# One decoder step on one core: place of the last pooling products, paired first groups of the output projection, earlier LayerNorm steps, another product for the mean, and new places for the operand order

## The chip, the cores and the metric

The kernel runs on one NeuronCore of a Trainium2 chip. The metric is the device time of one launch in microseconds (us), lower is better. Times are the median of several runs. A span is the time from the first to the last instruction of one profiled execution.

## What is computed

One layer of a hybrid decoder for a prompt of 256 positions and 8 sequences with 4 new positions each; both go through the same weights, so the kernel treats them as T = 288 columns. Cut to what matters:

```python
h = rmsnorm(x, norm1_g)
proj = h @ w_in + b_in                       # 2048 -> 1024 (a), 1024 (gate), 1024 (z)
u = a * sigmoid(gate)
c = silu(layernorm(depthwise_conv31(u) + conv_b) * ln_g + ln_b)   # mean, variance over 1024
d = multiscale_pool(z)                       # windows 2, 4, 8, 16; four groups of 256 channels
p = blockdiag(d, pool_w) * pool_scale        # four 256x256 products
x = x + concat(c, p) @ w_out
h2 = rmsnorm(x, norm2_g)
x = x + square(relu(h2 @ w_ff1)) @ w_ff2     # 2048 -> 8192 -> 2048
y = rmsnorm(x, norm_f)
```

Outputs are y and the new histories of u and z. All arrays are float32.

## The kernel before, in words

Channels lie on the 128 partitions, the 288 columns along the free axis. Every weight block (1024 rows by two times 128 columns) is loaded by SyncE's queue in two halves `wr` of 128x1024 (a ring of 6), and each half is split into `whi`, rounded to fp32r, and `wlo`, the rest (rings of 5). ScalarE (ACT) casts `whi` (L274), and VectorE (DVE, L279), GpSimd (POOL, L282) or a DMA (L277) forms `wlo`, by the table `WAYS`. The activations are split in the same way into a high and a low part. `gemm` (L310) then makes each result of three products: high by high, low weight by high, high weight by low. All products of the model go through `mm` (L302), so L305 is the line of nearly every matmul.

A tile of split activations has four rows of 288 numbers: the high parts of two neighbouring k are rows 1 and 2, the low parts rows 3 and 0. So (k + x) % 2, with x = 0 for the high and 1 for the low part, tells whether a product reads an odd or an even row. I call this the class of a product. The usual order in `gemm` alternates the classes 0, 1, 0, 1. A `gemm` called with `classes` takes the first products of its list in another order, so that their classes follow that string; `TURN` (L70), 48 digits long, is the one that is used. Before, five calls have it: the first two of the program, c5, and output group 2 of either half of `w_out`; the second group of `w_ff1` has it too, behind 12 products in the usual order.

The order of the groups of the input projection is `SEQUENCE` (L45): c0 to c7 are the conv columns (96 products each: 16 k, 2 halves, 3 kinds), p3 to p0 the pooling columns, and P3 to P0 the small products with `pool_w` (12 each). It ends in `p0 P1 c7 P0`. Then come 8 groups `g` of 256 output columns over the pooling half of `w_out` (48 products each), 8 over the conv half, and the two matrices of the MLP in four chunks.

While `chain` holds an instruction, every matmul is tied behind the one before it. At P1 (L540) it is cleared, and from there the scheduler of the tile framework places the matmuls by its own idea of time; it is filled again nowhere. `between` (L339) calls a function at the start of a given k. It puts the three LayerNorm steps on TensorE (PE) in the midst of groups 5, 6 and 7: `ln_mean` (L556, two float32 products with a matrix of ones), `ln_sums` (L561, which subtracts the mean, squares and sums on DVE and ACT and makes three products `pt` of one column), and `ln_rows` (L575, three products `pt` that spread the result to all partitions). DVE, ACT, POOL and SyncE each work in the order that the scheduler wrote. DVE's conv taps (`pc`, L461, 30 for each of 8 channel blocks) fill its gaps until the mean.

The conv result of c7 goes into `u_all` (L449), which reads the last PSUM (accumulator memory) tile `ac` of the input projection. The two tiles `ac` of the pool `acc` are used in turn, so an output group can't begin before the reader of the group two before it is done. The result of `pool_products(g)` is split by ACT (L514) and DVE (L515) into `dx`, the operand of the output projection.

Of the kernel before, what the change touches and what calls it, by code (L numbers as in the profile page):

```python
# [86 lines left out]
def trunk_kernel(ctx: ExitStack, tc: tile.TileContext, io):  # L87
# [222 lines left out]
    def gemm(banks, rhs, m_outer=False, between={}, classes="", by_part=False):  # L310
# [3 lines left out]
        gets = ready.pop(0)  # L314
# [9 lines left out]
        else:  # L324
            pairs = [(k, m) for k in range(0, n, 2) for m in range(len(banks))]
# [213 lines left out]
    for kind, i in SEQUENCE[3:]:  # L539
        if (kind, i) == ("P", 1):  # L540
            chain.clear()
        if kind == "c":
            conv_pair(i, conv_products(i, classes=TURN if i == 5 else ""))
        elif kind == "p":
            pool_group(i)
        else:
            pool_products(i)
    load_table(AF.Sqrt, f32(mixp[1][0])[:, 0:1])
# [6 lines left out]

    def ln_mean():  # L556
        norm["mean"] = ms("pmean")[:, 0, :T]
        mm(norm["mean"], ones, sum_c[:, 0, :], start=True, stop=False)
        return mm(norm["mean"], ones, cs[-1][:, 1, :], start=False, stop=True)

    def ln_sums():  # L561
        ssc = None
        for c in cs:
            nc.vector.tensor_tensor(c, c, norm["mean"][:, None, :].to_broadcast([P, 2, T]), op=ALU.subtract)
# [14 lines left out]
    BETWEEN = {5: {4: ln_mean}, 6: {6: ln_sums}, 7: {2: ln_rows}}  # L579
    behind = nullcontext()  # L580
    for g in range(8):
        bk = bank2()
        with behind:
            last = gemm(each(bk), [mixp[k] for k in korder], between=BETWEEN.get(g, {}), classes=TURN if g == 2 else "")
# [19 lines left out]
    last = None  # L604
    for g in range(8):
        bk = bank2()
        last = gemm(each(bk), mixc, classes=TURN if g == 2 else "")
# [30 lines left out]
    def second_rows():  # L638

        hl = actp.tile([P, 4, T], F32R, name="hl", tag="act")  # L640
        hi, lo = hl[:, 1, :], hl[:, 0, :]
        nc.scalar.copy(hi, ss2)
        nc.vector.tensor_tensor(lo, ss2, f32(hi), op=ALU.subtract)
        bk, r2 = ms("mean2"), row("r2")
        mean, root = bk[:, 0, :T], bk[:, 1, :T]
        mm(mean, means, hi, start=True, stop=False)
        last = mm(mean, means, lo, start=False, stop=True)
# [136 lines left out]
```

## Time and profile before

| what | value |
|---|---|
| median of 3 runs (lowest, highest) | 1084.95 us (1084.12, 1085.59) |
| span of the profiled execution | 1082.8 us |
| the execution's own time | not given by the page; the median of the runs is 2.15 us over the span |
| PE busy, matmuls | 1071.5 us (99%), 8198 |
| DVE, ACT, POOL busy | 635.4, 479.0, 173.6 us |
| mean granted TensorE clock | 0.997 |

A matmul's busy time (292 to 296 ns) overlaps that of its neighbours. The time that one adds is the distance between two starts. The chain of waits lists runs of matmuls with start, length and count, so length divided by count is that distance. A busy share of 99% therefore says little; small losses show as a longer distance or as a hole between two rows.

### The profile page before, as it was taken

Reading aid. Unit: us, or ns where it says so; the run is one execution under the profiler, and the core shown is the slowest. Engines: PE = TensorE matmul, PEld = TensorE weight load, DVE = VectorE, ACT = ScalarE, POOL = GpSimd, SP = SyncE. Lnnn points to the kernel's source line nnn. Section 1 sums busy time; section 2 is a strip of 40 time slices with the busy share of each in tenths; the row PEclk is TensorE's granted clock in tenths of the full one; section 3 lists DMA queues with packets and bytes.
Section 4 is the critical chain, followed back from the end, with each engine's and each line's share of the span. In section 5 each row is a group of like instructions: output and inputs, shape, how many; then the busy total and the mean of one; then the engine's idle time right before and its main releaser. Section 6 shows DMA issues by size and latency. Waiting matters only on the chain.

```text
span 1082.8 us, 19572 instructions
## 1 busy us (share of the span) xinstructions
PE 1071.5 (99%) x8198; PEld 1069.9 (99%) x8198; DVE 635.4 (59%) x818; ACT 479.0 (44%) x585; POOL 173.6 (16%) x180
## 2 busy tenths in 40 slices
PE   9999999999999999999999999999999999999996
PEld 9999999999999999999999999999999999999996
DVE  8899999678655544445544444545544445554553
ACT  8654445475544433334443333444433334444441
POOL 0878979512000000000000000000000000000001
PEclk9999999999999999999999999999999999999998
DMA  9896468545555555555555555555555555555522
GB/s 325 281 273 185 137 196 239 176 152 177 173 164 170 172 166 169 174 164 169 171 168 168 175 165 169 174 167 167 174 165 168 174 169 165 173 166 168 173 78 88
DMA packets 58296, 190.71 MB, mean 176 GB/s; under 512 B 6240, under 2 KB 11232, under 8 KB 58208
## 3 DMA queue, kind: packets, MB, share of 16 engines
q1 hardware_dynamic: 56336, 184.35, 53.9%
q0 software_dynamic: 1008, 3.67, 1.9%
q8 instruction: 64, 1.05, 0.4%
q10 hardware_dynamic: 864, 1.44, 0.4%
q14 instruction: 24, 0.20, 0.1%
HBM read 185.16 MB, written 4.28 MB: 175 GB/s over the span
## 4 chain that ended last, share of the span: by engine, by line
PE 77%; issue 20%; ACT 1%; DVE 0%; DMA 0%; POOL 0%; POOLq 0%
PE ac L305 77%; PE pp L305 1%; DMA wr<-in_w 0%; ACT whi L274 0%; POOL xT L720 0%; ACT n L595 0%; DVE wlo L279 0%; PE pt L305 0%; PE pmean L305 0%; POOLq L770 0%; DVE xT L695 0%; DVE n L592 0%; ACT whi L364 0%; ACT mx L597 0%; DVE hx L367 0%
## 5 line engine op out<-in xcount | busy, mean ns | idle before, releaser
L274 ACT CAST whi<-wr 128x1024 fp32r<-128x1024 f32 (+1 forms) x332 | 348.0, 1049 | 551.4 <-PE ac L305 533.5
L279 DVE TENSOR_TENSOR wlo<-wr,whi 128x1024 fp32r<-128x1024 f32 x288 | 353.1, 1226 | 348.5 <-ACT whi L274 348.5
L305 PE MATMUL ac<-ax,whi 128*128 128x288 f32 x2048 | 351.0, 292 | 0.0
L305 PE MATMUL ac<-fx,whi 128*128 128x288 f32 x2048 | 350.2, 292 | 0.0
L305 PEld LDWEIGHTS ac<-ax,whi 128*128 128x128 f32 x2048 | 296.0, 187 | 0.0
L305 PEld LDWEIGHTS ac<-fx,whi 128*128 128x128 f32 x2048 | 295.6, 187 | 0.0
L305 PE MATMUL ac<-ax,wlo 128*128 128x288 f32 x1024 | 217.4, 292 | 0.0
L305 PE MATMUL ac<-fx,wlo 128*128 128x288 f32 x1024 | 216.4, 292 | 0.0
L305 PEld LDWEIGHTS ac<-ax,wlo 128*128 128x128 f32 x1024 | 162.6, 187 | 0.0
L305 PEld LDWEIGHTS ac<-fx,wlo 128*128 128x128 f32 x1024 | 162.3, 187 | 0.0
L305 PE MATMUL ac<-hx,whi 128*128 128x288 f32 x768 | 131.8, 295 | 1.2 <-DVE hx L367 1.2
L720 POOL TENSOR_TENSOR xT<-xT,rf 128x288 f32<-128x288 f32 x4 | 3.1, 795 | 800.1 <-ACT rf L724 800.1
L305 PEld LDWEIGHTS ac<-hx,whi 128*128 128x128 f32 x768 | 112.1, 190 | 1.4 <-ACT hx L369 1.4
L282 POOL TENSOR_TENSOR wlo<-wr,whi 128x512 fp32r<-128x512 f32 x74 | 100.3, 1410 | 35.3 <-ACT whi L274 34.3
L461 DVE SCALAR_TENSOR_TENSOR pc<-u_all,vec,pc 128x256 f32<-128x256 f32 x232 | 99.5, 483 | 1.9 <-ACT pc L458 0.7
L305 PE MATMUL ac<-hx,wlo 128*128 128x288 f32 x384 | 80.1, 294 | 0.0
L305 PEld LDWEIGHTS ac<-hx,wlo 128*128 128x128 f32 x384 | 61.1, 190 | 0.0
L305 PE MATMUL ac<-dx,whi 128*128 128x288 f32 x256 | 46.0, 296 | 0.0
L305 PE MATMUL ac<-mx,whi 128*128 128x288 f32 x256 | 45.1, 294 | 0.1
L664 DVE SCALAR_TENSOR_TENSOR t<-ac,r 128x576 f32<-128x576 f32 x32 | 24.2, 758 | 25.1 <-PE ac L305 25.1
L305 PEld LDWEIGHTS ac<-dx,whi 128*128 128x128 f32 x256 | 38.0, 188 | 0.2
L305 PEld LDWEIGHTS ac<-mx,whi 128*128 128x128 f32 x256 | 37.5, 188 | 0.6 <-ACT mx L597 0.4
(133 smaller groups left out, 533.6 us busy)
## 6 DMA issues: line engine op xcount, KB each, us to landing
wr<-in_w SPq DMA_DIRECT2D x335, 512.0 KB, 3.8
wlo<-in_w POOLq DMA_DIRECT2D x7, 512.0 KB, 7.7
xT<-in_xT SPq DMA_DIRECT2D x8, 288.0 KB, 7.3
wr<-in_w SPq DMA_DIRECT2D x5, 256.0 KB, 3.6
out_u_out<-u_all SPq DMA_DIRECT2D x1, 1208.0 KB, 9.3
u_all<-in_hist_c SPq DMA_DIRECT2D x8, 136.0 KB, 6.2
out_z_out<-z_all SPq DMA_DIRECT2D x1, 668.0 KB, 9.9
z_all<-in_hist_p SPq DMA_DIRECT2D x4, 152.0 KB, 7.5
```

The lines of the kernel that those rows point to most:

```text
L274: nc.scalar.copy(hi, raw)
L279: nc.vector.tensor_tensor(lo, raw, f32(hi), op=ALU.subtract)
L282: nc.gpsimd.tensor_tensor(lo[:, j : j + 2, :], raw[:, j : j + 2, :], f32(hi[:, j : j + 2, :]), op=ALU.subtract)
L305: last = nc.tensor.matmul(*args, **kw)
L461: nc.vector.scalar_tensor_tensor(out=dst, in0=up[:, w : w + SEQ], scalar=cwv[:, w : w + 1], in1=pc, op0=ALU.mult, op1=ALU.add)
L664: nc.vector.scalar_tensor_tensor(out=t, in0=bk[:, :, :T], scalar=0.0, in1=both(rows2[0]), op0=ALU.max, op1=ALU.mult)
L720: eng.tensor_tensor(xk, xk, r[:, None, :].to_broadcast([P, n, T]), op=ALU.mult)
```

## The change

- `SEQUENCE` is walked without P1 and P0. P1 is called inside c7, before k = 12. P0 is called inside the first output groups. `chain` is now cleared only behind these.
- Output groups 0 and 1 of the pooling half are one `gemm` over four accumulators: 36 products of group 0 (all that don't need P0), P0, then the 36 of group 1, and the 24 that use P0's result; the last 60 have `TURN` on their first 48.
- Groups 0 and 1 of the conv half are likewise one `gemm`, with k outermost and `TURN` on the first 48 products; they are tied behind group 7's last product.
- `ln_mean` moves from k = 4 to k = 0 of group 5, `ln_sums` from k = 6 to k = 4 of group 6, `ln_rows` from k = 2 to k = 0 of group 7. Groups 5 and 7 get `TURN`, group 2 of the pooling half loses it.
- The mean: DVE adds the last two parts, ACT rounds the sum, DVE forms the rest, and two fp32r products with `means` (ones divided by 2048) replace the two float32 products; the subtraction becomes a scalar_tensor_tensor with factor -2.
- The weights' list `ready` may run one group further ahead (`ahead`). In `second_rows` the root lies in SBUF rather than PSUM.

```diff
-        gets = ready.pop(0)
+        gets = gets or ready.pop(0)
...
-                if m == 0:
-                    begins[len(todo)] = k
+                begins[len(todo)] = (k, m) if m else k
...
-            todo[j] = next(p for p in head if (p[0] + p[3]) % 2 == int(c))
+            todo[j] = next(p for p in head if c == "." or (p[0] + p[3]) % 2 == int(c))
...
-    for kind, i in SEQUENCE[3:]:
+    for kind, i in SEQUENCE[3:-1]:
         if (kind, i) == ("P", 1):
-            chain.clear()
+            continue
         if kind == "c":
-            conv_pair(i, conv_products(i, classes=TURN if i == 5 else ""))
+            conv_pair(i, conv_products(i, classes=TURN if i == 5 else "", **(dict(gets=ahead(1), between={12: lambda: pool_products(1)}) if i == 7 else {})))
...
+    early = [(k, m) for k in (0, 2, 4) for m in range(4)]
+    early.sort(key=lambda km: km[1] // 2)
+    gemm(each(bks[0]) + each(bks[1]), proj, gets=[lambda k, m: both_gets[m // 2][0](k, m % 2)], between={(0, 2): lambda: pool_products(0)}, classes="." * 36 + TURN, pairs=early + [(6, m) for m in range(4)])
+    chain.clear()
...
+    def mean_rows(total, name):
+        hl = actp.tile([P, 4, T], F32R, name=nm("hl"), tag="act")
+        hi, lo = hl[:, 1, :], hl[:, 0, :]
+        nc.scalar.copy(hi, total)
+        nc.vector.tensor_tensor(lo, total, f32(hi), op=ALU.subtract)
+        mean = ms(name)[:, 0, :T]
+        mm(mean, means, hi, start=True, stop=False)
+        return mean, mm(mean, means, lo, start=False, stop=True)
...
-        mm(norm["mean"], ones, sum_c[:, 0, :], start=True, stop=False)
-        return mm(norm["mean"], ones, cs[-1][:, 1, :], start=False, stop=True)
+        nc.vector.tensor_tensor(total, total, cs[-1][:, 1, :], op=ALU.add)
+        norm["half"], last = mean_rows(total, "pmean")
...
-    BETWEEN = {5: {4: ln_mean}, 6: {6: ln_sums}, 7: {2: ln_rows}}
+    BETWEEN = {5: {0: ln_mean}, 6: {4: ln_sums}, 7: {0: ln_rows}}
...
-            last = gemm(each(bk), [mixp[k] for k in korder], between=BETWEEN.get(g, {}), classes=TURN if g == 2 else "")
+                last = gemm(each(bk), proj, between=BETWEEN.get(g, {}), classes=TURN if g in (5, 7) else "")
...
+    chain.append(last)
+    gemm(each(bks[0]) + each(bks[1]), mixc, gets=[lambda k, m: two_gets[m // 2][0](k, m % 2)], classes=TURN)
+    chain.clear()
```

How the instructions stand on PE near P1, before. `ac` is the accumulator of c7, `hx` its operands, `pp` the accumulator of P1:

```order
L305 MATMUL ac_2089<-hx_215,whi_2075 128x288
L305 MATMUL pp_2044<-dx_1877,whi_2023 128x288 x2
L305 MATMUL pp_2044<-dx_1877,wlo_2024 128x288 x2
L305 MATMUL ac_2089<-hx_215,whi_2075 128x288
L305 MATMUL ac_2089<-hx_227,whi_2080 128x288 x2
L305 MATMUL ac_2089<-hx_227,wlo_2081 128x288 x2
L305 MATMUL ac_2089<-hx_227,whi_2080 128x288
L305 MATMUL pp_2044<-dx_1877,whi_2023 128x288 x4
L305 MATMUL pp_2044<-dx_1877,wlo_2024 128x288 x2
L305 MATMUL pp_2044<-dx_1877,whi_2023 128x288 x2
```

The same place now:

```order
L305 MATMUL ac_2072<-hx_215,whi_2062 128x288 x2
L305 MATMUL pp_2145<-dx_1877,whi_2023 128x288 x2
L305 MATMUL pp_2145<-dx_1877,wlo_2024 128x288 x2
L305 MATMUL pp_2145<-dx_1877,whi_2023 128x288 x4
L305 MATMUL pp_2145<-dx_1877,wlo_2024 128x288 x2
L305 MATMUL pp_2145<-dx_1877,whi_2023 128x288 x2
L305 MATMUL ac_2072<-hx_227,whi_2067 128x288 x2
```

P1 was cut in two and lay between the products of a pair of k, so two neighbours had the same class at either cut. Now it stands whole between two pairs of k, and the classes alternate through it.

DVE behind c7's result, before (`tg` is the gate of c7, `dx` of `pp` the operand made from P0's result, `pc` and `c` conv taps):

```order
L449 SCALAR_TENSOR_TENSOR u_all<-ac_2089,vec,tg_2194 128x256
L449 SCALAR_TENSOR_TENSOR u_all<-ac_2089,vec,tg_2194 128x8x4
L461 SCALAR_TENSOR_TENSOR pc_1061<-u_all,vec,pc_1061 128x256
L515 SCALAR_TENSOR_TENSOR dx_2041<-pp_2233,vec,dx_2041 128x288
L461 SCALAR_TENSOR_TENSOR pc_1061<-u_all,vec,pc_1061 128x256 x2
L461 SCALAR_TENSOR_TENSOR pc_1718<-u_all,vec,pc_1718 128x256
L515 SCALAR_TENSOR_TENSOR dx_2041<-pp_2233,vec,dx_2041 128x288
```

The same place now:

```order
L448 SCALAR_TENSOR_TENSOR u_all<-ac_2072,vec,tg_2206 128x256
L448 SCALAR_TENSOR_TENSOR u_all<-ac_2072,vec,tg_2206 128x8x4
L460 SCALAR_TENSOR_TENSOR pc_1061<-u_all,vec,pc_1061 128x256 x2
L460 SCALAR_TENSOR_TENSOR pc_1718<-u_all,vec,pc_1718 128x256
L460 SCALAR_TENSOR_TENSOR pc_1061<-u_all,vec,pc_1061 128x256
L460 SCALAR_TENSOR_TENSOR pc_1718<-u_all,vec,pc_1718 128x256
L460 SCALAR_TENSOR_TENSOR pc_1061<-u_all,vec,pc_1061 128x256
L514 SCALAR_TENSOR_TENSOR dx_2041<-pp_2297,vec,dx_2041 128x288
L460 SCALAR_TENSOR_TENSOR pc_1718<-u_all,vec,pc_1718 128x256
L460 SCALAR_TENSOR_TENSOR pc_1061<-u_all,vec,pc_1061 128x256
L465 TENSOR_REDUCE c_1717<-prd_2241 128x32
L460 SCALAR_TENSOR_TENSOR pc_1718<-u_all,vec,pc_1718 128x256
L514 SCALAR_TENSOR_TENSOR dx_2041<-pp_2297,vec,dx_2041 128x288
```

The two operands from P0 stand behind nine conv taps and a reduction; before, one stood behind one tap and the other behind three more.

DVE where the conv half begins, before (`mx` are its operands, `n` the normalized parts, `ac` the last result of the pooling half):

```order
L279 TENSOR_TENSOR wlo_2896<-wr_2889,whi_2895 128x1024
L587 TENSOR_TENSOR xT<-xT,ac_2744 128x576
L598 TENSOR_TENSOR mx_2813<-n_2809,mx_2813 128x2x288
L598 TENSOR_TENSOR mx_2820<-n_2816,mx_2820 128x2x288
L592 TENSOR_TENSOR n_2823<-c_1060,pt_2705 128x576
```

The same place now:

```order
L622 TENSOR_TENSOR mx_2829<-n_2825,mx_2829 128x2x288
L616 TENSOR_TENSOR n_2839<-c_1060,pt_2711 128x576
L279 TENSOR_TENSOR wlo_2821<-wr_2814,whi_2820 128x1024
L622 TENSOR_TENSOR mx_2836<-n_2832,mx_2836 128x2x288
L611 TENSOR_TENSOR xT<-xT,ac_2760 128x576
L616 TENSOR_TENSOR n_2846<-c_1717,pt_2711 128x576
```

The first operands `mx` are now made before group 7's sum instead of behind it. The orders of POOL and SyncE are unchanged, and that of PE is again the same from output group 2 of the conv half on.

More of the change, by code (lines that the diff above doesn't have):

```diff
@@ L324, in gemm @@
         else:
[L325 removed]
+            pairs = pairs or [(k, m) for k in range(0, n, 2) for m in range(len(banks))]
             if m_outer:
@@ L638, in second_rows @@
     def second_rows():
[L640 to L647, printed above, removed]
+        r2, root = row("r2"), tmp("q")
+        mean, last = mean_rows(ss2, "mean2")
         nc.scalar.activation(root, mean, AF.Sqrt, bias=eps)
```

27 lines of the change are left out of this document (19 added, 8 removed).

## The prediction

> **What bounds the kernel now.** I read the page's first part, then the chain of waits in order of time, then the timelines of PE and DVE between 150 and 240 us, where the orders of the two programs differ.
>
> ```profile
> span 1082.8 us, 19572 instructions
> PE 1071.5 (99%) x8198; PEld 1069.9 (99%) x8198; DVE 635.4 (59%) x818; ACT 479.0 (44%) x585; POOL 173.6 (16%) x180
> ```
>
> TensorE is the bound, so a change can win only what PE loses between products. The chain shows how much that is; each row is start, length, line, count.
>
> ```profile
> 36.65 73.54 PE ac L305 x564
> ...
> 111.75 24.96 PE ac L305 x192
> 136.71 1.56 PE pp L305 x12
> 138.27 21.71 PE ac L305 x167
> 159.98 0.53 PE pp L305 x4
> ...
> 162.34 6.26 PE ac L305 x47
> 168.60 1.60 PE pp L305 x12
> 170.20 31.10 PE ac L305 x236
> 201.31 0.97 PE pmean L305 x4
> 202.28 4.87 PE ac L305 x37
> ...
> 219.55 64.96 PE ac L305 x492
> 284.51 0.26 PE mean L305 x2
> 284.77 572.63 PE ac L305 x4404
> ```
>
> The reader should divide. 24.96 us for 192 is 130.0 ns a product, 21.71 for 167 is 130.0, 572.63 for 4404 is 130.0. But 6.26 for 47 is 133.2, right after P1 (`pp`) was cut into c7. The shape is the same, so there are two paces. The first row holds two passes of `TURN` and is 0.22 us over 564 x 130 ns: a pass costs at most 0.11 us, and the pace after it is 130 ns. The pooling product at 136.71, whole and between groups, did not break the pace; the cut one did, and it came back only behind `TURN` in output group 2. DMA load does not explain it:
>
> ```profile
> DMA  9896468545555555555555555555555555555522
> ```
>
> A slice is 27 us; the slow rows from 202 to 232 lie in the eighth and ninth slices, with shares of 0.5 and 0.4, no more than in the MLP, which goes at 130 ns.
>
> **What PE loses from 159.98 to 284.51, against 130 ns.** From 159.98 to 201.31 are 41.33 us for 313 products (4, 6, 8, 47, 12, 236), or 40.69: loss 0.64. The mean takes 0.97. From 202.28 to 219.55 are 17.27 us for 120 products of the output (24, 48, 48), 15.60, and the two `pt` steps. These rows of PE's timeline price the steps and the waits:
>
> ```profile
> 170.84 0.97 PE L305 MATMUL ac<-dx,whi 128*128 128x288 f32 x5
> 171.64 0.42 PE L305 MATMUL ac<-dx,wlo 128*128 128x288 f32 x2
> ...
> 210.11 0.59 PE L305 MATMUL pt<-ones,q 128*96 128x1 f32 x6
> 210.56 0.51 PE L305 MATMUL ac<-dx,whi 128*128 128x288 f32 x2
> 210.91 0.42 PE L305 MATMUL ac<-dx,wlo 128*128 128x288 f32 x2
> ...
> 213.82 0.80 PE L305 MATMUL pt<-ident,st 96*128 96x96 f32 x6
> 214.41 0.51 PE L305 MATMUL ac<-dx,whi 128*128 128x288 f32 x2
> 214.76 0.43 PE L305 MATMUL ac<-dx,wlo 128*128 128x288 f32 x2
> ...
> 219.00 0.43 PE L305 MATMUL ac<-dx,whi 128*128 128x288 f32 x2
> 219.55 0.54 PE L305 MATMUL ac<-mx,whi 128*128 128x288 f32 x2
> 219.93 0.43 PE L305 MATMUL ac<-mx,wlo 128*128 128x288 f32 x2
> ...
> 221.85 0.70 PE L305 MATMUL ac<-mx,whi 128*128 128x288 f32 x4
> ```
>
> The `pt` steps take 210.91 - 210.11 less two products, 0.54, and 214.76 - 213.82 less two, 0.68: 1.22 in all, and the loss there is 17.27 - 15.60 - 1.22 = 0.45. Of it, 0.29 is the wait for the first `mx` (two products take 0.26; the next starts 0.55 after 219.00). From 219.55 to 284.51, 492 products need 63.96, so 1.00 is lost: 0.48 up to 221.85 (2.30 us for 14 products), the rest to the slow pace until `TURN` in group 2. The sum: 0.64 + 0.45 + 1.00 = 2.09, plus what the mean can save.
>
> **The mean.** Two fp32r products take 0.26 (row 284.51); the four passes now take 0.97: saving 0.71. In front of them come a cast and two DVE operations; the same cast and rest in the MLP have
>
> ```profile
> L643 DVE TENSOR_TENSOR hl<-ss,hl 128x288 fp32r<-128x288 f32 x1 | 0.5, 450 | 0.0
> L642 ACT CAST hl<-ss 128x288 fp32r<-128x288 f32 x1 | 0.4, 427 | 0.0
> ```
>
> so 0.45 + 0.43 + 0.45 = 1.33 us. The last conv result, and DVE's next work:
>
> ```profile
> 195.80 0.48 DVE L461 SCALAR_TENSOR_TENSOR c<-u_all,vec,pc 128x256 f32<-128x256 f32 x1
> 198.22 0.76 DVE L587 TENSOR_TENSOR xT<-xT,ac 128x576 f32<-128x576 f32 x1 [1.94 <-PE ac L305]
> ```
>
> It is done at 196.28, the operands of the mean at 197.6, and group 5 begins about 198.2 (group 4's sum waits for its end): 0.6 us of cover, with the 1.94 us hole on DVE. If it fails, PE waits as long as it is late. DVE's rest waits for ACT's cast; behind it stands only group 4's sum, which waits for PE anyway. The changed subtraction has one pass over the same 576 columns as before, about its 0.75 us, and lies beside PE. `ln_sums` and `ln_rows` come 1.56 us earlier on PE, and the mean 3.1 us earlier, so the step from mean to sums keeps a group and a half; the price of the `pt` steps stays 1.22. Between them 24 products run at the slow pace, 24 x 3.2 ns = 0.08.
>
> **TURN.** Five passes in this stretch, where two were: the losses above hold those two, so all five are charged new, 5 x 0.11 = 0.55. Between them PE goes at 130 ns.
>
> **The places that are now set.** c7 begins at 138.27 + 96 x 0.130 = 150.75. With P1, 36 products of group 0 and P0 that is 156 products, so P0 ends at 171.03. The next product writes the tile that `u_all` reads:
>
> ```profile
> 170.58 0.64 DVE L449 SCALAR_TENSOR_TENSOR u_all<-ac,vec,tg 128x256 f32<-128x256 f32 x2
> 171.13 0.48 DVE L461 SCALAR_TENSOR_TENSOR pc<-u_all,vec,pc 128x256 f32<-128x256 f32 x1
> 171.52 0.51 DVE L515 SCALAR_TENSOR_TENSOR dx<-pp,vec,dx 128x288 fp32r<-128x288 f32 x1
> 171.95 1.39 DVE L461 SCALAR_TENSOR_TENSOR pc<-u_all,vec,pc 128x256 f32<-128x256 f32 x3
> ...
> 175.63 1.22 DVE L466 TENSOR_REDUCE c<-prd 128x32 f32<-128x1024 f32 x1
> 176.76 0.87 DVE L461 SCALAR_TENSOR_TENSOR pc<-u_all,vec,pc 128x256 f32<-128x256 f32 x2
> ...
> 219.47 0.76 DVE L587 TENSOR_TENSOR xT<-xT,ac 128x576 f32<-128x576 f32 x1 [0.33 <-PE ac L305]
> ```
>
> DVE has the same work up to there, so `u_all` ends at about 171.22 again. Today PE stops at that point for 0.14 us (five products from 170.84 to 171.64). It will come earlier and wait 0.2, and a product behind a wait costs more: the two at 219.55 took 0.38 rather than 0.26. I take 0.24 + 0.11 = 0.35. Everything on PE stands behind it, but it lies ahead of `TURN`, so the pace survives it.
>
> Next, the second operand of P0's result. From 171.13 DVE does six taps, `dx`, two taps, the reduction, a tap and `dx`. A tap takes 0.39 (0.87 less the overlap, for two) or 0.48 where it waits for the one before; the reduction takes 1.13 to the next start, `dx` 0.43. Nine taps at 0.39 are 3.51, with 1.13 and 0.86 that makes 5.50: ready at 176.6, or at 177.2 with seven taps at 0.48. By PE's order it is needed 42 products behind P0: 171.03 + 0.35 + 42 x 0.132 = 176.9. So the wait lies between 0 and 0.3 plus 0.11 for the restart; I take 0.25. It falls six products before `TURN` ends. If the pace is lost there, group 1's rest to group 5 go slow: 157 products x 3.2 ns = 0.50.
>
> At the head of the conv half the first operands are ready earlier, since DVE makes them ahead of group 7's sum; 0.29 goes, and with k outermost over four accumulators a further operand is needed every 3.1 us rather than 1.56. But the second accumulator waits for group 7's sum, which starts at best 0.34 after the last product's start (219.13 to 219.47), takes 0.76, and stands behind a `wlo` and an `mx`. PE gets there 12 products, 1.6 us, after the start: a wait of 0 to 0.6; I take 0.20 with the restart.
>
> The weights' list runs one group further ahead, but the rings and the orders of SyncE and POOL are the same, so no transfer moves by that.
>
> **The sum.** Lost now and recoverable: 2.09 + 0.71 = 2.80. Lost after: 0.55 + 0.08 + 0.35 + 0.25 + 0.20 = 1.43. Gain 1.4 us. The span goes from 1082.8 to 1081.4; with the 2.15 us around it left alone, the median from 1084.95 to 1083.55.
>
> One rule of the Trainium skill speaks against the larger part. Its page "TensorE: Matmul & The Clock Gate", section "Step-by-step: what each phase is for", says that loading the next weights takes no read bandwidth from the running matmul and that throughput is purely the number of columns; by that the order of the reads changes no pace. The rows 133.2 against 130.0 at one shape disagree, so its outcome, the time of rival one, has 0.05 of that rival's 0.20.
>
> **Rivals.** A difference of 0.2%, 2.2 us, is about the least that a measurement of this kernel can tell from no change.
>
> - One, the order brings nothing, or the wait at 176.9 breaks the pace and `TURN` does not hold it. Then only 0.71 and the waits of 0.14, 0.29 and 0.48 can go, 1.62, less the new waits of 0.80: gain 0.8, 1084.1. For it: the first wait stands just ahead of `TURN`, the second inside it. Against it: every pass of `TURN` in the chain is followed by 130 ns.
> - Two, nothing waits at the set places but for `u_all`: lost after is 0.55 + 0.08 + 0.35 = 0.98, gain 1.8; with 0.09 a pass and 0.1 for `u_all` it is 0.63, gain 2.2, 1082.8. DVE's taps would have to run at 0.39 throughout.
> - Three, slower: the pace of the MLP. If the second group of `w_ff1` no longer ends in 130 ns, the 4404 products of the long row take 133.2: 14 us, 1097.6. It decides from 3.6 / 0.0032 = 1130 slow products on, about 150 us. Against it: PE's order there is unchanged, and its `TURN` stands behind the step `second_rows`, which is the same on PE.
>
> That the change doesn't do what it says is excluded by the order: the pooling products stand whole and alternate.
>
> **How the numbers follow.** Forecast 0.60; rival one 0.20; rival two 0.15; rival three 0.05. The likeliest time is 1083.55. The low end is rival two with the runs' own scatter, 1082.5; the high end is rival one with both uncertain waits at their upper ends (0.25 to 0.41, 0.20 to 0.71; gain 0.1), 1084.85. Faster by over 0.2% means below 1082.78: rival two for the most part, and the edge of the forecast, 0.16. Slower by over 0.2% is rival three and a little for waits that I don't see, 0.06. The rest, 0.78, is within.
>
> **What would show it.** Right: c7, P1 and P0 in rows of 130 ns up to 171; a hole of 0.2 to 0.4 us at 171; the row of the mean at 0.26; 130 ns from group 1 to 5; the first `mx` with no hole. Wrong: a pace of 133 ns between 177 and 198 (rival one), no hole at 171 (rival two), 133 ns behind 285 (rival three), or a hole ahead of the mean or the `pt` rows, which I count as covered.

## The result and the profile after

| | before | after |
|---|---|---|
| median of 21 runs each (lowest, highest), us | 1084.88 (1083.54, 1086.17) | 1086.16 (1084.78, 1087.54) |
| span of the profiled execution, us | 1082.8 | 1083.9 |
| mean granted TensorE clock | 0.997 | 0.995 |

The ratio is 1.0013, with a 95% interval from 1.0007 to 1.0019: after is slower by 0.13%, 1.3 us, where the prediction had a gain of 1.4 us and a range that ended at 1084.85. The profiled execution's own time is 1085.87 us. Two executions, one of 2566.53 us (e11) and one of 1783.39 us (before, beside e5 to e8), were in a slow state and are left out of the medians and ratios below.

The page's first part, for after:

```profile
span 1083.9 us, 19570 instructions
PE 1070.2 (99%) x8196; PEld 1068.5 (99%) x8196; DVE 641.3 (59%) x820; ACT 478.1 (44%) x586; POOL 174.6 (16%) x180
```

These lines hide it: PE is busy for 1.3 us less than before in a span that is 1.1 us longer, and DVE has two instructions more but 5.9 us more of busy time. Where, the chain of waits of after shows (start, length, engine, tile, line, count):

```profile
159.57 1.56 PE pp L305 x12
161.13 7.80 PE ac L305 x60
168.93 1.56 PE pp L305 x12
170.49 20.39 PE ac L305 x156
...
194.25 4.32 DVE sum_c L580
...
198.59 0.44 ACT hl L572
...
199.08 1.10 PE pmean L305 x2
200.18 10.61 PE ac L305 x72
210.79 0.43 PE pt L305 x6
211.22 3.29 PE ac L305 x24
214.51 0.64 PE pt L305 x6
215.15 70.53 PE ac L305 x540
285.67 0.26 PE mean L305 x2
285.93 572.63 PE ac L305 x4404
```

Divide again. 7.80 for 60 is 130.0 ns, and 20.39 for 156 is 0.11 over 156 x 130: the slow stretch of before is gone, and one pass of `TURN` is what is left. 70.53 for 540 is 0.33 over, three passes. The MLP is unchanged, 572.63. But the chain leaves PE for DVE and ACT between 190 and 199: there PE stood still. The timelines of DVE, POOL, ACT and PE of after around it:

```profile
193.67 0.48 DVE L460 SCALAR_TENSOR_TENSOR c<-u_all,vec,pc 128x256 f32<-128x256 f32 x1
194.25 4.31 DVE L580 TENSOR_TENSOR sum_c<-sum_c,c 128x288 f32<-128x288 f32 x1
199.06 0.46 DVE L573 TENSOR_TENSOR hl<-sum_c,hl 128x288 fp32r<-128x288 f32 x1 [0.50 <-ACT hl L572]
```

```profile
190.75 7.50 POOL L282 TENSOR_TENSOR wlo<-wr,whi 128x512 fp32r<-128x512 f32 x6
200.05 2.53 POOL L282 TENSOR_TENSOR wlo<-wr,whi 128x512 fp32r<-128x512 f32 x2 [1.81 <-ACT whi L274]
```

```profile
194.15 1.05 ACT L274 CAST whi<-wr 128x1024 fp32r<-128x1024 f32 x1 [2.19 <-PE ac L305]
198.59 0.43 ACT L572 CAST hl<-sum_c 128x288 fp32r<-128x288 f32 x1 [3.39 <-DVE sum_c L580]
198.93 1.04 ACT L274 CAST whi<-wr 128x1024 fp32r<-128x1024 f32 x1
```

```profile
196.68 0.42 PE L305 MATMUL ac<-dx,whi 128*128 128x288 f32 x2
199.08 1.10 PE L305 MATMUL pmean<-hl,means 128*128 128x288 f32 x2 [1.97 <-ACT hl L572]
199.98 0.45 PE L305 MATMUL ac<-dx,whi 128*128 128x288 f32 x1
...
202.62 0.45 PE L305 MATMUL ac<-dx,whi 128*128 128x288 f32 x2
```

The sum of the last two parts of the mean (L580) took 4.31 us. The rest behind it (L573), of the same shape and form, took 0.46. The sum started in the middle of POOL's unbroken run of six instructions, which ended at 190.75 + 7.50 = 198.25, and ended 0.31 later, at 198.56. ACT's cast and DVE's rest then put the operands at 199.5.

PE's bill: its last product started at 196.81 and the next was due at 196.94; it came at 199.08, 2.14 late. The two products of the mean took 0.90 up to the next start, not 0.26: 0.64, since the second of them waited for the rest besides and the clock was already lower. And 11 products from 199.98 to 202.62 took 2.64, 0.24 each, not 0.13: 1.21. Together 3.99 us. What slowed the products, the table by stretch says; it gives the busy time of PE, PEld, DVE, ACT and POOL, and then PE's granted clock:

```profile
196.00:200.00 4.00, 2.03 (x12) 1.49 (x11) 3.50 (x3) 1.38 (x2) 2.24 (x2) 0.90 0.58 174
200.00:204.00 4.00, 4.00 (x23) 4.00 (x23) 3.86 (x7) 2.03 (x3) 2.53 (x2) 0.67 0.41 121
```

Behind the hole the granted clock fell: 0.67 from 200 to 204, and a product at 0.24 us is close to half the pace of 0.13.

For the experiments I use, beside the medians, a length in the profiled execution that the scatter of the program's start doesn't touch: from the first product of P1 (`pp` at 159.57 above) to the row of `mean` in the MLP. All kernels do the same work there but for the mean. After: 285.67 - 159.57 = 126.10. Before: 284.51 - 159.98 = 124.53, less 0.13, since P1 stood one product earlier: 124.40. So after loses 1.70 there. Less the 3.99, the rest of the change gained 2.3. A length is of one execution of each kernel; after, e13 and e14, which differ only in the form of one or two instructions, lie within 0.4 us.

### The profile page after: what moved, and what is told of

Its sections match the earlier page's. It is cut to its first block, busy times and chain, and to the rows that moved or that the text cites. A ratio compares the mean times of both kernels' runs of the same rounds, so it can differ in the third digit from the quotient of the medians.

```text
span 1083.9 us, 19570 instructions
## 1 busy us (share of the span) xinstructions
PE 1070.2 (99%) x8196; PEld 1068.5 (99%) x8196; DVE 641.3 (59%) x820; ACT 478.1 (44%) x586; POOL 174.6 (16%) x180
## 4 chain that ended last, share of the span: by engine, by line
PE 77%; issue 20%; DVE 1%; DMA 1%; ACT 0%; SPq 0%; POOL 0%; POOLq 0%; DVEq 0%
PE ac L305 76%; DMA wr<-in_w 1%; PE pp L305 1%; DVE sum_c L580 0%; PE pt L305 0%; POOL xT L743 0%; DVE pc L460 0%; DVE z_all L419 0%; SPq L191 0%; ACT z_all L417 0%; DVE wlo L372 0%; PE pmean L305 0%; ACT whi L363 0%; ACT hx L368 0%; SPq L187 0%
```

## The experiments

Theory A: that one event is the whole miss; DVE's sum, with both operands in SBUF, waits for POOL's run, and PE pays for it twice, by the hole and by the clock. B: the new places by themselves cost. C: the sum is slow by itself. The length is from P1 to `mean` as above.

| kernel | median us | ratio to before (95%) | P1, `mean` at | length |
|---|---|---|---|---|
| before | 1084.88 | | 159.98, 284.51 | 124.40 |
| after | 1086.16 | 1.0013 (1.0007, 1.0019) | 159.57, 285.67 | 126.10 |
| e1 old mean | 1083.09 | 0.9984 (0.9975, 0.9992) | 159.44, 282.28 | 122.84 |
| e2 short run of POOL | 1083.48 | 0.9984 (0.9975, 0.9993) | 160.40, 283.18 | 122.78 |
| e3 mean at k = 4 | 1085.20 | 1.0004 (0.9996, 1.0013) | 160.04, 284.24 | 124.20 |
| e4 sum in PSUM | 1082.40 | 0.9977 (0.9968, 0.9986) | 160.93, 283.28 | 122.35 |
| e5 steps at before's places | 1084.49 | 0.9998 (0.9989, 1.0007) | 159.76, 283.77 | 124.01 |
| e6 new mean alone | 1085.04 | 1.0003 (0.9994, 1.0012) | 160.63, 285.09 | 124.33 |
| e7 e4, conv half unpaired | 1082.85 | 0.9983 (0.9975, 0.9992) | 160.70, 283.07 | 122.37 |
| e8 e4, no TURN in the first pair | 1082.97 | 0.9988 (0.9979, 0.9997) | 159.93, 282.91 | 122.98 |
| e9 e4, steps at before's places | 1084.42 | 0.9997 (0.9988, 1.0006) | 160.02, 283.85 | 123.83 |
| e10 cast on DVE | 1088.78 | 1.0036 (1.0023, 1.0048) | 160.74, 288.69 | 127.95 |
| e11 e4, mean at k = 2 | 1084.88 | 1.0001 (0.9992, 1.0010) | 160.40, 284.45 | 124.05 |
| e12 pooling part alone | 1084.44 | 0.9996 (0.9987, 1.0004) | 160.65, 284.53 | 123.88 |
| e13 sum and rest in the other form | 1085.86 | 1.0014 (1.0005, 1.0023) | 159.14, 285.51 | 126.37 |
| e14 the sum alone in it | 1085.83 | 1.0013 (1.0005, 1.0022) | 160.55, 286.55 | 126.00 |
| e15 POOL in finer pieces | 1093.06 | 1.0081 (1.0067, 1.0094) | 159.58, 292.83 | 133.25 |

Before's medians beside the experiments lay between 1084.61 and 1084.87. e6 has P1 cut as in before, so 0.13 is taken off there too.

### e1, the old mean put back

The sum, cast, rest and fp32r products go; two float32 products as before, at k = 0:

```diff
-        nc.vector.tensor_tensor(total, total, cs[-1][:, 1, :], op=ALU.add)
-        norm["half"], last = mean_rows(total, "pmean")
+        mm(norm["mean"], ones, sum_c[:, 0, :], start=True, stop=False)
+        return mm(norm["mean"], ones, cs[-1][:, 1, :], start=False, stop=True)
```

> The changed kernel with the two float32 products of the old mean put back at k = 0 of group 5, so without the sum, the cast and the rest that now come first on DVE and ACT. Theory A (the loss is one event: DVE's sum for the mean, both operands in SBUF, stands 4.3 us instead of 0.46 while POOL runs six tensor_tensor without a break; PE waits for it and goes at half clock for 3.4 us after): no hole ahead of the mean, no stretch of 240 ns products, about 3.9 us less plus 0.7 for the float32 products, 1083.0 us, or 0.998 of the kernel before. Theory B (the new places and orders cost time themselves, and the hole only hides another wait): 1085 us or more.

1083.09, as A has it. Faster than before by 0.16%: the rest of the change is a gain of 1.6 us, and its new places cost nothing by themselves. B falls.

### e2, a shorter run of POOL

The second `wlo` of one block of weights goes to DVE, so that POOL's run around the sum has four instructions, not six:

```diff
-"w0": "VV", "w": "GG"
+"w0": "VV", "w6": "GV", "w": "GG"
```

> The changed kernel with one more half block's low part given to DVE instead of POOL (second half of output group 6), so POOL's run of six tensor_tensor at 190.8 us has four and ends about 195.8. Theory A: the sum for the mean ends within 0.4 us of the end of that run, about 196.1, and takes 1.8 us instead of 4.3; the rest comes behind the low part on DVE, PE waits about 0.9 us; 1083 to 1084 us. Theory C (the sum is slow by itself, in place on a tile that POOL wrote): 4.3 us again, and 1086 us.

1083.48, in A's range. The timelines of DVE and POOL of e2:

```profile
195.09 1.80 DVE L580 TENSOR_TENSOR sum_c<-sum_c,c 128x288 f32<-128x288 f32 x1
```

```profile
191.52 5.04 POOL L282 TENSOR_TENSOR wlo<-wr,whi 128x512 fp32r<-128x512 f32 x4
```

POOL's run ends at 196.56, the sum at 196.89, 0.33 behind it, as in after. The sum was not touched and took 1.80 for 4.31: C falls.

### e3, the mean four k later

```diff
-    BETWEEN = {5: {0: ln_mean},
+    BETWEEN = {5: {4: ln_mean},
```

> The changed kernel with the mean's products back at k = 4 of group 5, 24 products or 3.1 us later on PE; nothing else moves. Theory A: the sum takes 4 us as before, but is done by about 198.6 and its rest by 199.6, and PE gets there about 200.1: no hole, no half clock; 1082.3 us, if the sums at group 6 are still in time. Theory B: 1085 us or more, with the loss in another wait.

1085.20, a miss of A's number; B's number and its "loss in another wait" came out. The sum took 4.30 again, and there was no hole at the mean, as expected; but the next step on the chain was late in its place. PE's timeline of e3, at the sums of group 6:

```profile
209.15 0.64 PE L305 MATMUL pt<-ones,q 128*96 128x1 f32 x6 [1.75 <-DVE q L594]
```

A hole moved down the chain by one step. I had counted the cover at the mean only. The later place of the mean is enough for that, without the long sum: e11 below has a short sum and nearly the same hole. After's own places are not at fault, as e1 and e4 show.

### e4, the sum formed in PSUM

ACT copies one part into the bank of the mean, and DVE adds the other there, so that the sum and the rest each have one operand in PSUM:

```diff
+        nc.scalar.copy(total, cs[-1][:, 1, :])
-        nc.vector.tensor_tensor(total, total, cs[-1][:, 1, :], op=ALU.add)
+        nc.vector.tensor_tensor(total, total, sum_c[:, 0, :], op=ALU.add)
```

where `total` is now `ms("pmean")[:, 1, :T]`.

> The changed kernel with the last conv result copied to PSUM by ACT first, and the sum for the mean formed there, so that DVE's sum and its rest have one operand in PSUM and one in SBUF; the mean stays at k = 0. Theory A in its narrow form (two operands in SBUF are what collides with POOL): the sum takes about 0.5 us while POOL's run goes on, PE waits 0.3 us or less, 1082.3 to 1082.8 us. If any DVE operation that reads SBUF collides, the sum takes 3 us or more and the time stays near 1086.

1082.40, 0.23% under before and the fastest of all. DVE and POOL of e4:

```profile
196.96 0.47 DVE L582 TENSOR_TENSOR pmean<-pmean,sum_c 128x288 f32<-128x288 f32 x1 [1.46 <-ACT pmean L581]
```

```profile
192.03 10.16 POOL L282 TENSOR_TENSOR wlo<-wr,whi 128x512 fp32r<-128x512 f32 x8
```

The same sum in the midst of POOL's run, even a longer one, takes 0.47. With one operand in PSUM the sum did not wait for POOL. The mean's saving comes out as well: e4's length is 0.49 under e1's. The rest of the 0.71 is a short wait at the mean, whose two products take 0.49 in e4's chain and not 0.26.

### e5, the three steps back at before's places

The mean is as in after.

```diff
-    BETWEEN = {5: {0: ln_mean}, 6: {4: ln_sums}, 7: {0: ln_rows}}
+    BETWEEN = {5: {4: ln_mean}, 6: {6: ln_sums}, 7: {2: ln_rows}}
```

> The kernel after with the three LayerNorm steps back at the places of before (mean four k into group 5, sums six k into group 6, rows two k into group 7); the fp32r mean, its sum from SBUF, the pooling places and the pairs stay. Theory A (VectorE's sum is kept out until GpSimd's unbroken run is over; TensorE loses only where it stands at the mean or at a step fed by it): the sum again takes about 4.3 us and ends 0.3 us behind GpSimd's run, but no hole of more than 0.3 us at the mean (the operands are there at about 199.9, its place is about 200.5), and the sums, needed 1.56 us later than in the run with the mean alone put back, stand without a hole of more than 0.4 us: 1082.8 to 1083.6. Theory B (the long sum throws VectorE's chain back for good, wherever the steps stand): the sums are still about 1.7 us late, 1085. Theory C (the new places by themselves cost, the long sum nothing): the sum is short here, 1082.4.

1084.49, between A's and B's numbers. No hole at the mean, 0.16 at the sums, but one at the second of the mixed operands, where PE waited for `mx`. Whether the long sum or the places did that, e5 can't tell; e9 does.

### e6, before with the new mean alone

```diff
-        mm(norm["mean"], ones, sum_c[:, 0, :], start=True, stop=False)
-        return mm(norm["mean"], ones, cs[-1][:, 1, :], start=False, stop=True)
+        nc.vector.tensor_tensor(total, total, cs[-1][:, 1, :], op=ALU.add)
+        norm["half"], last = mean_rows(total, "pmean")
```

> The kernel before with the fp32r mean alone (sum of the two partial sums on VectorE from SBUF, cast, rest, two products, subtraction with the factor), at its old place and with all else as before. Theory A: GpSimd's run lies there from 191.93 to 201.97, so the sum that starts at about 196.3 ends at 202.3, the operands are there at 203.1 where the place of the mean is 201.3: a hole of about 1.8 us and a stretch at half clock of up to 1.7 us, less the 0.71 that the two products save: 1086.5 to 1088. Theory B (the mean is only late because it was moved up): the saving alone, 1084.1.

1085.04, neither. DVE, POOL and PE of e6:

```profile
197.06 3.43 DVE L568 TENSOR_TENSOR sum_c<-sum_c,c 128x288 f32<-128x288 f32 x1
```

```profile
192.61 7.56 POOL L282 TENSOR_TENSOR wlo<-wr,whi 128x512 fp32r<-128x512 f32 x6
```

```profile
210.62 0.64 PE L305 MATMUL pt<-ones,q 128*96 128x1 f32 x6 [0.59 <-DVE q L582]
```

The sum is long here too, and again ends 0.32 behind POOL's run (200.49 and 200.17). But the run has six instructions, where it had eight in before, so the mean was in time, and the price came at the sums. I had taken the run's length from before, without the change's own hand in it: ACT's next cast of weights now stands behind the cast of the sum, so POOL runs out of work. Length 124.33 against 124.40: at before's place the new mean brings nothing, since the 0.71 that it saves on PE is given back one step later.

### e7, the first two groups of the conv half apart again

e4, and there:

```diff
-    gemm(each(bks[0]) + each(bks[1]), mixc, gets=[lambda k, m: two_gets[m // 2][0](k, m % 2)], classes=TURN)
...
-        if g > 1:
-            last = gemm(each(bk), mixc, classes=TURN if g == 2 else "")
+        last = gemm(each(bk), mixc, classes=TURN if g == 2 else "")
```

> The kernel after with the sum of the mean formed in a bank of PSUM (the best version so far, 1082.4), and the pair of the first two groups of the second projection taken apart again as in before. The prediction's sum: the hole of 0.29 at the first mixed operand, 0.48 up to 2.3 us behind it and 0.5 of slow pace until the pass in the third group come back, less one pass of 0.09: 1083.5. Rival (the pair moves nothing, because VectorE is behind in both): 1082.4.

1082.85. The medians differ by 0.45, with intervals that overlap (0.9983 and 0.9977); the lengths differ by 0.02. In e7's trace the first `mx` has no hole either. So in the profile the pair moves nothing, and the rival of this run holds; a few tenths in the time stay open.

### e8, no TURN in the first pair of output groups

e4, and there:

```diff
-classes="." * 36 + TURN, pairs=early
+pairs=early
```

> The same best version without the pass of TURN in the pair of the first two groups of the first projection, the orders of the products there natural. Pace theory (a pass is needed behind the last pooling products to come back to 130 ns): 133 ns from the last pooling products to the pass in the sixth group, some 200 products by 3.2 ns, 0.65 less the 0.09 of the pass: 1083.0. Rival (the pace is not broken by pooling products that stand whole, the pass is idle): 130 ns throughout, 1082.3.

1082.97, length 0.63 over e4's, as the pace theory has it (0.56). The row behind P0 in the chain, first of e8, then of e4:

```profile
170.85 27.32 PE ac L305 x204
```

```profile
171.85 26.61 PE ac L305 x204
```

27.32 over 204 is 133.9 ns, 26.61 is 130.4. But the place where the pace breaks is another than I thought. In e8's timeline of PE the 130 ns go on behind P0 until this row, where PE waits 0.16 for the second operand from P0:

```profile
176.04 0.80 PE L305 MATMUL ac<-dx,whi 128*128 128x288 f32 x4
```

The row before it has its last start at 175.76, so 0.29 lie between the two starts, and the next distance is 0.24. From there it is 133 ns until the pass in group 5. So the pace breaks at the product that waited, and not at the pooling products, which stand whole. That the wait broke it rests on this one place.

### e9, e4 with the steps at before's places

```diff
-    BETWEEN = {5: {0: ln_mean}, 6: {4: ln_sums}, 7: {0: ln_rows}}
+    BETWEEN = {5: {4: ln_mean}, 6: {6: ln_sums}, 7: {2: ln_rows}}
```

> The best version so far (after with the sum of the mean in PSUM, 1082.4), with the three LayerNorm steps back at the places of before. Theory D (moving the steps up is what makes the first mixed operands early enough): the wait for the first mixed operands of before comes back, 0.3 to 0.5 with the restart, and the next operands another 0.5, less 0.2 for the short wait at the mean: 1083.0 to 1083.3. Rival (the steps' places are indifferent as long as the sum is short, and the long sum alone made the mixed operands late in the run with the places of before): 1082.2 to 1082.4, no hole over 0.2 us between 216 and 222.

1084.42, the length 1.48 over e4's: D by its kind, and more than its number. PE and DVE of e9:

```profile
219.83 0.40 PE L305 MATMUL ac<-mx,whi 128*128 128x288 f32 x1 [0.73 <-DVE mx L629]
```

```profile
218.35 0.76 DVE L618 TENSOR_TENSOR xT<-xT,ac 128x576 f32<-128x576 f32 x1 [0.32 <-PE ac L305]
219.02 1.42 DVE L629 TENSOR_TENSOR mx<-n,mx 128x576 fp32r<-128x576 f32 x2
```

Here `mx` stands behind group 7's sum (`xT`), which waits for PE; in e4 it stands at 216.39, ahead of that sum. With a short sum e9 loses what e5 loses, so in e5 it was the places and not the long sum. To have moved the steps up is worth 1.5 us once the pair is there; the 0.73 above is the largest piece of it.

### e10, the cast of the sum on DVE

If ACT's cast queues POOL's next work behind it, then to free ACT makes POOL's run longer:

```diff
-        nc.scalar.copy(hi, total)
+        (nc.vector.tensor_copy if name == "pmean" else nc.scalar.copy)(hi, total)
```

> The kernel after with the cast of the sum for the mean on VectorE in place of ScalarE, so that ScalarE's next cast of weights is not held behind it. Theory A: GpSimd's run in after ended at 198.25 only because ScalarE's next cast stood behind the cast of the sum; with ScalarE free that cast comes at about 197.1, the run goes on with two more pieces to 200.8, VectorE's sum takes 6.5 to 6.9 us in place of 4.3, TensorE's hole at the mean grows from 2.0 to about 4.5, and the time is 1088.0 to 1089.0, slower than after though no engine got more work of weight. Should the run break for a moment at 198.2, the sum slips in there and the time is that of after, 1086.2. Theory C (the sum is slow by itself or waits for ScalarE): 1086.0 or below, the sum at 4.3 us or shorter.

1088.78, in A's range, but not wholly by A's way. DVE and POOL of e10:

```profile
195.42 4.28 DVE L580 TENSOR_TENSOR sum_c<-sum_c,c 128x288 f32<-128x288 f32 x1
199.74 1.25 DVE L572 CAST hl<-sum_c 128x288 fp32r<-128x288 f32 x1
201.03 1.40 DVE L573 TENSOR_TENSOR hl<-sum_c,hl 128x288 fp32r<-128x288 f32 x1
```

```profile
195.63 3.75 POOL L282 TENSOR_TENSOR wlo<-wr,whi 128x512 fp32r<-128x512 f32 x3
199.43 1.39 POOL L282 TENSOR_TENSOR wlo<-wr,whi 128x512 fp32r<-128x512 f32 x1
```

POOL's run went on as expected, but with a pause of 0.05 us, from 199.38 to 199.43, where ACT's cast was just late; within the run the records of neighbours overlap instead. The sum got in there and ended at 199.70. Then the cast and the rest each waited out one more instruction of POOL. The operands were complete 7.0 us after the sum's start, in after 5.3, and the length is 1.85 over after's: an edit that moved one cast from ACT to DVE, and so let POOL's run go on, made the kernel slower. The sum itself was no longer than in after.

### e11, e4 with the mean two k later

```diff
-    BETWEEN = {5: {0: ln_mean},
+    BETWEEN = {5: {2: ln_mean},
```

> The best version so far with the mean two k into its group instead of ahead of it. The short wait at the mean (two starts of 0.24 where 0.13 is the pace) goes, 0.2, and the sums keep over a us of cover: 1082.2. Rival (the sums become late as in the run with the mean four k in): a hole of more than 0.5 us at 208, 1083.

1084.88, later than the rival's 1083, and the rival's hole was 1.68 us at the sums. DVE of e11 ahead of it:

```profile
206.28 0.74 DVE L618 TENSOR_TENSOR xT<-xT,ac 128x576 f32<-128x576 f32 x1
...
207.61 1.21 DVE L279 TENSOR_TENSOR wlo<-wr,whi 128x1024 fp32r<-128x1024 f32 x1
208.75 0.44 DVE L601 TENSOR_TENSOR q<-q 128x288 f32<-128x288 f32 x1
```

The last sum of squares (`q`) now stands on DVE behind group 5's `xT` and a `wlo`; a mean 1.56 us later made the sums 1.7 us late by this order. The steps have less room than the holes at the mean suggest.

### e12, the pooling part alone

After, with the mean, the LayerNorm places, the passes in groups 5 and 7 and the conv half all as in before.

```diff
-    BETWEEN = {5: {0: ln_mean}, 6: {4: ln_sums}, 7: {0: ln_rows}}
+    BETWEEN = {5: {4: ln_mean}, 6: {6: ln_sums}, 7: {2: ln_rows}}
...
-                last = gemm(each(bk), proj, between=BETWEEN.get(g, {}), classes=TURN if g in (5, 7) else "")
+                last = gemm(each(bk), proj, between=BETWEEN.get(g, {}), classes="")
```

with the edits of e1 and e7 beside it.

> The pooling part of the change alone: last pooling products at set places, first two groups of the first projection as a pair with its pass of TURN; mean, LayerNorm places, passes in groups six and eight and the second projection as before. The prediction's terms: of the 0.64 lost up to the mean all comes back less one pass of 0.09 and no waits (the trace of after shows none): gain 0.5; of the loss behind it nothing comes back: 1084.1 to 1084.3. Rival (the new order of the first groups also makes VectorE's chain earlier, and so the mixed operands): a hole of less than 0.2 us at the first mixed operand and 1083.5.

1084.44, and 0.52 in length: the prediction's term for this part (0.64 less a pass) and no more.

### e13 and e14, the sum in another form

Conv taps on DVE, `scalar_tensor_tensor`, were never delayed by POOL (0.48 each in all traces). Is it the form? e13 has the sum and the rest in it, e14 the sum alone:

```diff
-        nc.vector.tensor_tensor(total, total, cs[-1][:, 1, :], op=ALU.add)
+        nc.vector.scalar_tensor_tensor(out=total, in0=total, scalar=1.0, in1=cs[-1][:, 1, :], op0=ALU.mult, op1=ALU.add)
```

> The kernel after with the sum and the rest for the mean as scalar_tensor_tensor (times one, plus; times minus one, plus) in place of tensor_tensor, operands in SBUF as before. In all traces so far the taps, which have this form and two operands in SBUF, take 0.48 while GpSimd runs. Theory A2 (it is the form tensor_tensor that is kept out during GpSimd's run): the sum takes 0.5, the rest 0.5, the operands are there at about 195.8, no hole at the mean, half clock gone: 1082.0 to 1082.5. Theory A1 (any instruction with two operands in SBUF that isn't yet started when GpSimd's run is on): the sum takes 4 us as before, 1086.

> The same with the sum alone as scalar_tensor_tensor and the rest as tensor_tensor. Theory A2: the sum takes 0.5, and the rest, which starts at about 195.4 in the middle of GpSimd's run, takes the wait instead: it ends 0.3 behind the end of the run, at 198.5 if the run breaks where ScalarE's cast is just late, at 201.1 if it does not; hole at the mean of 1.7 to 4.3 us: 1085.2 to 1088.8. Rival (the sum is long for a reason of its own, such as the operand that GpSimd wrote last): the rest takes 0.46, 1082.3.

1085.86 and 1085.83, A1's time; A2 falls. DVE of e13:

```profile
193.83 4.26 DVE L580 SCALAR_TENSOR_TENSOR sum_c<-sum_c,c 128x288 f32<-128x288 f32 x1
```

The form made no difference. I had been wrong about the taps: their `pc` lies in PSUM (the pool `cvp`), so they have one operand in SBUF, like the sum in e4. The rest took 0.46 in e14, as its rival has it, but POOL stood still by then, so that says nothing. That the operand which POOL wrote last is not enough by itself shows e4, whose sum reads it too. A1's wide wording, any instruction with two operands in SBUF, is more than these runs show; the next section has rows against it.

### e15, POOL in finer pieces

```diff
-            for j in range(0, raw.shape[1], 2):
-                nc.gpsimd.tensor_tensor(lo[:, j : j + 2, :], raw[:, j : j + 2, :], f32(hi[:, j : j + 2, :]), op=ALU.subtract)
+            step = 1 if way == "g" else 2
+            for j in range(0, raw.shape[1], step):
+                nc.gpsimd.tensor_tensor(lo[:, j : j + step, :], raw[:, j : j + step, :], f32(hi[:, j : j + step, :]), op=ALU.subtract)
```

with `"w": "gg"` in the table.

> The kernel after with GpSimd's remainders of the weights of this stage in pieces of 256 columns in place of 512, the same run of work in twice as many instructions. Theory A (the sum is kept out as long as GpSimd's instructions follow without a pause, however many they are): the sum again takes about 4.3 us and ends 0.3 behind the end of the run: 1086.0 to 1086.8. Theory E (it is let in after so many of GpSimd's instructions, three or four): it takes 2.0 to 2.6 us, the hole is 0.3 at most: 1083 to 1084.

1093.06; the mechanism is A's, the time is neither's. DVE and POOL of e15:

```profile
198.90 5.72 DVE L581 TENSOR_TENSOR sum_c<-sum_c,c 128x288 f32<-128x288 f32 x1 [0.83 <-POOL sum_c L472]
```

```profile
198.06 0.81 POOL L472 TENSOR_TENSOR sum_c<-sum_c,c 128x288 f32<-128x288 f32 x1
198.81 5.50 POOL L283 TENSOR_TENSOR wlo<-wr,whi 128x256 fp32r<-128x256 f32 x8
```

Eight instructions passed before the sum got in; it ended 0.31 behind their end at 204.31. So it is not let in after so many of them: E falls. The time rose for a reason that I had not priced: POOL's own last add to `sum_c` came at 198.06, where it came at 189.98 in after. Some 5 us of that is POOL's order, which the edit changed: between its last three adds stand eight pieces of 256 twice, in after two of 512 twice, so two more halves of a block come first. Most of the rest is that POOL was slower with more instructions (5.50 for two halves of a block, which take 5.04 in e2).

## Why the prediction missed

**The step that failed** is the mean: "so 0.45 + 0.43 + 0.45 = 1.33 us", and from it "0.6 us of cover". I gave DVE's sum the 0.45 of a row in the MLP, taken at a moment when POOL had nothing to do, and set it into a stretch where POOL runs without a pause. It took 4.31. Shown by e2 (a shorter run, a shorter sum), e4 (the same run, one operand in PSUM, 0.47) and e15 (a longer sum behind more instructions); in after, e2, e6 and e15 the sum ended 0.31 to 0.33 behind the end of POOL's run, whatever its length. The places were not the fault: DVE had the last conv result at 194.15 and PE got to the mean at 196.94, so by an estimate with my 1.33 us the cover would have been about 1.4.

A row could have warned me. Before, the groups by form of DVE have the same form, shape and types twice, once beside POOL's work (three of the four) and once without:

```profile
L503 DVE TENSOR_TENSOR dx<-d,dx 128x576 fp32r<-128x576 f32 x4 | 5.0, 1246 | 0.0
L598 DVE TENSOR_TENSOR mx<-n,mx 128x576 fp32r<-128x576 f32 x4 | 2.9, 755 | 0.2 <-ACT mx L597 0.2
```

1246 ns and 755 ns. The Trainium skill has the reason, page "SBUF — State Buffer", section "Who interferes with whom": a VectorE instruction with two inputs in SBUF contends with a GpSimd instruction that reads SBUF, and one with at most one SBUF input, outside the modes that take two ports, does not. The sum agrees in every run here, 4.31 against 0.47. The page also has the one that starts first hold the ports for the whole instruction; by that the sum would have waited for the one instruction of POOL under way, 1.3 us at most, and PE's hole would have been small or none. The measured wait went on through three further instructions in after and seven in e15, up to a pause.

Nor is that the rule in these traces. Before, one of the four `dx` above began 0.44 us into a run of six instructions of POOL, and took 1.47. DVE and POOL of before:

```profile
164.91 1.47 DVE L503 TENSOR_TENSOR dx<-d,dx 128x576 fp32r<-128x576 f32 x1
```

```profile
164.47 8.09 POOL L282 TENSOR_TENSOR wlo<-wr,whi 128x512 fp32r<-128x512 f32 x6 [1.77 <-ACT whi L274]
```

It ended at 166.38, with 6.2 us of the run to go: it got in behind the first instruction, as the page has it, and that run of six took 0.6 longer than after's. In after the sum of squares `q` at 206.26 did the same (1.36 us). In all 17 traces 187 such instructions (`wlo`, `dx`, `z_all`, `q`) began beside an instruction of POOL with another close behind, and each got in at the next boundary. Only the sum for the mean was passed over, in each run that forms it in SBUF. So that it waited for POOL's run is shown; why it alone missed the boundaries stays open.

**"If it fails, PE waits as long as it is late"** was too small as well: the hole was 2.14, and the wait for the rest and the lower clock behind it cost another 1.85.

**The other terms**, each against its row:

- The slow pace (0.64 up to the mean, part of the 2.09): right; e12 measured 0.52 for the pooling part, and `TURN` at 0.11 a pass is what the rows of after show. e8 shows that the pass in the pair was needed, 0.63, but the pace breaks at a wait, not at P0's place.
- The wait for `u_all`, 0.35: not there. In after DVE had it done at 170.00, 10.43 behind P1's start, and PE needed it at 170.33. I had kept before's distance, 171.22 - 159.98 = 11.24. Why DVE was 0.8 earlier I didn't test.
- The second operand of P0, 0.25: none in after, where DVE had it at 175.64. The cover is thin: in e8, by another order of the products, that wait is there (0.16 and the slow restart).
- The second accumulator of the conv half, 0.20: no hole in after.
- The holes at the first `mx` (0.29 and 0.48): gone, as forecast. I gave the credit to the earlier operands and the pair; e9 and e7 give it to the steps alone (1.48 against 0.02).
- The saving at the mean, 0.71: 0.49 in e4, where a short wait of 0.23 is left.

**The rivals.** None was it. Rival two's price, a gain of 2.2, is what e4 shows without the stall (2.3), and its reason, "nothing waits at the set places but for `u_all`", is right for them; not even `u_all` was waited for. That it gave the mean the same free passage as my forecast made both wrong in the same place. What I listed last as wrong, "a hole ahead of the mean", had a line but no price. That 0.2% is about the least that one can tell was too cautious: with 21 runs each the interval reaches 0.06% either way.

The account by lengths: the pooling part 0.52 (before to e12), the earlier steps with the conv half's pair and the passes in groups 5 and 7 1.04 (e12 to e1), the new mean 0.49 if its sum has an operand in PSUM (e1 to e4), and a loss of 3.26 as it was written (e1 to after). To sum up, a gain of 1.56 and a loss of 3.26: 1.70.

## What to carry to other kernels

Take the price of an instruction from a row in the same company: for a DVE instruction with both operands in SBUF, look up what POOL does at that time. Give it at least the rest of POOL's instruction under way, and as an upper bound the time to the end of POOL's run, which is what the sum took here. If it is on the way to TensorE, form it with one operand in PSUM, where the sum took 0.47. And when a step on a chain is moved, count the cover at each later step too, by DVE's order: three runs put the hole one step further down (e3, e6, e11).

## What the runs showed of the hardware

- Back-to-back instructions of POOL kept DVE's sum out through as many as eight of them; in e10 it got in at a pause of 0.05 us. A cast got in after one instruction, without a pause, in the same run (1.25 us), and so did 187 other instructions with two operands in SBUF over all traces. What decides between the two I didn't find.
- A hole of 1.97 us on PE (after) was followed by a lower granted clock (0.67 from 200 to 204); behind holes of 1.75 (e3) and 1.68 (e11) it stayed at 1.00. The Trainium skill, page "TensorE: Matmul & The Clock Gate", section "Part 1: The HAM clock gate", has the clock fall after an idle window of about 3.4 us; here less than that sufficed.
- An engine off the path set the length of the stall: POOL's run in after ended because ACT's next cast of weights stood behind the very cast that waited for the sum. With ACT free the run went on, and the cast and the rest waited in place of the sum (e10, 1.85 longer).
- The two paces of PE at one shape, 130 and 133 ns: in e8 the change from the one to the other comes at a wait of 0.16 us, and a pass of `TURN` turns it back (130.4 a product in e4, 133.9 in e8 without it).
